# w_down in a tuned encoder block: the sums of the staying operands on VectorE, the first splits of a change behind the last bank's copy

## The chip, the cores and the metric

The kernel runs on one core of a Trainium2 chip. The metric is the device time of one execution in microseconds; the time of a kernel is the median of its runs. The core has TensorE (PE) for matrix products, VectorE (DVE), ScalarE (ACT) and GpSimd (POOL) for work on rows of elements, and SyncE (SP), which here only issues DMAs. Each engine works through its own queue in order; semaphores hold an instruction back until what it needs is there.

## The reference

One layer of an encoder: an attention group and a Fourier group share an input and an output projection, then a gated MLP follows. Everything is float32, with 2048 positions, a model width of 1024 and a hidden width of 2816. What matters here is the MLP:

```python
h = rmsnorm(x, g_ffn[l])
up = centred_dwconv(h @ w_up[l], w_conv[l], b_conv[l])
gate, val = up[..., :D_FF], up[..., D_FF:]
x = x + (jax.nn.silu(gate) * val) @ w_down[l]
return rmsnorm(x, g_final)
```

`centred_dwconv` is a convolution of width 3 over the positions, for each channel by itself.

## The kernel before

**Products of float32.** The matmuls here take operands of the type float32r. Every float32 operand is split into a high part of that type and a low part, and a product is three matmuls: high by high, high by low, low by high (`mm3`, lines 127 to 129). `split` makes the parts: line 83 copies the high part on ScalarE, line 84 subtracts it on VectorE (or on another engine that is named) to get the low part, and so follows line 83.

**The up products.** The product of 1024 columns of `h` with `w_up` is done by a scheme of Strassen's kind: blocks of two by two are combined by sums, seven products (p1, p5, p6, p2, p7, p4, p3) are made instead of eight, and their results are combined in three PSUM banks for each of the 22 steps n: bank a takes p1, p6, p7 and p4 one after the other, bank d p5 and p3, bank c p2. `exec_up` copies or adds a bank into a row buffer (`xg` for the gate, `xv` for the value) after a product, with ScalarE (line 979) and VectorE (line 980). A product that follows in the same bank must wait until the copy has read it. As a rule the order is p7 of step n, p1 of step n+1, p4 and p3 of step n; the last step of a half has no p1 behind its p7. After p4 the convolution of the value part follows, after p3 that of the gate part (lines 1007 to 1009), then `silu` and the product of the two parts (1014, 1015), which is stored to DRAM (`gd`). This is done twice: grp 0 for the first 1024 positions, grp 1 for the others.

**The w_down products.** The 22 blocks of hidden channels are shared out: blocks 0 to 9 are multiplied directly in rounds (`fil`, `exec_fil`; rnd 0 to 2, and rnd 3 at the end), the other twelve in two groups of six by the same seven-product scheme (`dn`, `exec_dn`). In a round, eight banks of PSUM collect ten steps n, each with a gate block and two weight blocks (tile `d`), 24 matmuls in a step. The sequence is: up grp 0, round 0, up grp 1, round 1, dn 0, round 2, dn 1, round 3.

**The staying operands.** In the seven-product scheme one side stays for a whole phase: seven tiles `b` (one for each product) with a high and a low part. Before up grp 1 they have to be made anew from `h` (four block rows, kb 0 to 3), before dn 0 and dn 1 from `w_down` (three block rows each). `b_part` makes one block row: four loads from DRAM into a buffer of the tag `xg` and one of the tag `xv` (two buffers each, shared with the up products' row buffers; tile `hb`), four sums (`sums` with `second=True`, lines 840 to 843: three new tiles of the tag `sum`, which has three buffers, and one sum in place), and seven splits into `b`. It is called from `exec_fil` at every second step n of the rounds 0, 1 and 2, so ten times. In the kernel before, the four sums are on GpSimd (`nc.gpsimd`), the low parts on VectorE. Two other users of `sums` have theirs on VectorE: `prep_a` and, before the first up products, `b_pieces`.

**What sets the order.** A planner puts the instructions of each engine in an order: it goes through the program with estimates of its own for durations and takes, for an engine that is free, the ready instruction that comes first in the program. On the chip the order is fixed. So an instruction whose input comes later than estimated holds up all that is behind it on its engine. `issue_after(r, prev)` adds an edge for the planner that puts `r` behind `prev`; without `wait` no semaphore is made for it.

**Operands of the rounds.** `flow` prepares operands ahead of use: nine ring buffers (`ring`), of which a step of a round takes three, so the operands of a step are written when the third step before it is done. The loads of a step need one of two stage buffers.

Of the kernel before, what the change touches and what calls it, by code (L numbers as in the profile page):

```python
# [40 lines left out]
class Block:  # L41
# [808 lines left out]
    def b_part(self, grp, kb, out):  # L850


        nc = self.nc

        st = [self.mp.tile([P, S // 2 + 3], F32, tag=tag, bufs=2, name=f"hb{grp}_{kb}{tag}")[:, :2 * HALF]
              .rearrange("p (k c) -> p k c", k=2) for tag in ("xg", "xv")]
        for half in range(2):
            if grp < 2:
                src = self.htd[kb + 4 * half, :, grp * S // 2:(grp + 1) * S // 2]
            else:  # L860
                f = self.FT + self.CH * (grp - 2) + kb + self.NK * half
                src = self.a["w_down"][f * P:(f + 1) * P, :]
            for i in range(2):
                nc.sync.dma_start(st[i][:, half], src[:, i * HALF:(i + 1) * HALF])
        x11, x21, x12, x22 = (st[i // 2][:, i % 2] for i in range(4))
        t1, t2, t3, t4 = self.sums(self.sp, (x11, x21, x12, x22), f"hs{grp}_{kb}", nc.gpsimd, True)
        for o, v in zip(out, (x11, t1, t2, x21, t3, t4, x22)):
            self.split(v, o[:, 0, kb], o[:, 1, kb])

    def b_pieces(self, out):  # L870

# [90 lines left out]
    def exec_up(self, grp, n, q, o):  # L962
        nc, p = self.nc, self.mp
        ps = self.product(q, f"u{grp}_{n}", o)
        W1 = S // 2 + 3
        at = 1 if grp == 0 else 2
        c = [slice(at, at + HALF), slice(at + HALF, at + 2 * HALF)]
        if q == "p1":
            for part, nm in enumerate(("xg", "xv")):
                f = n + NF * part  # L970
                xb = p.tile([P, W1], F32, tag=nm, bufs=2, name=f"{nm}{grp}_{n}")
                self.xb[n, nm] = xb
                if grp == 0:
                    nc.gpsimd.memset(xb[:, 0:1], 0.0)
                else:
                    nc.gpsimd.memset(xb[:, W1 - 1:], 0.0)  # L976
                    nc.gpsimd.tensor_copy(xb[:, 0:2], self.carry[:, f, :])
        xg, xv = self.xb[n, "xg"], self.xb[n, "xv"]
        copy = lambda o, i: nc.scalar.activation(o, i, AF.Copy)
        add = lambda o, i: nc.vector.tensor_tensor(o, i, o, ALU.add)  # L980
        if q == "p1":
            copy(xg[:, c[0]], ps)
        elif q == "p6":
            copy(xg[:, c[1]], ps)
        elif q == "p2":
            add(xg[:, c[0]], ps)
        elif q == "p7":
            copy(xv[:, c[1]], ps)
            add(xv[:, c[1]], self.banks[f"u{grp}_{n}", "d"])
        elif q == "p4":  # L990
            copy(xv[:, c[0]], ps)
            self.conv(grp, n, 1)
        elif q == "p3":
            add(xg[:, c[1]], ps)
            self.conv(grp, n, 0)
            self.gate(grp, n)
# [275 lines left out]
```

## Time and profile before

| | |
|---|---|
| median of three runs | 2517.06 us (2513.75 to 2518.77) |
| the profiled execution | 2513.03 us, span 2511.2 us |
| TensorE busy | 2456.5 us |
| VectorE busy | 1771.0 us |
| ScalarE busy | 1298.3 us |
| GpSimd busy | 791.8 us |

The span is the time from the first to the last instruction in the trace. Times within the trace are counted from its start. A matmul's duration in the trace is modelled, and neighbours overlap, so the distance of their starts is what tells how TensorE gets on. A row of a timeline has in brackets how long the engine was idle before the instruction and what ended that. The granted clock is a share of TensorE's full 2.4 GHz; 0.5 of it is its other level, 1.2 GHz.

### The profile page before, as it was taken

The numbers are of one execution on the slowest core, as the hardware profiler recorded it, in microseconds if no ns is written. First come the engines' busy times: TensorE is split into PE (matmuls) and PEld (weight loads), VectorE is DVE, ScalarE is ACT, GpSimd is POOL, SyncE is SP. The second block draws the span as 40 slices with busy tenths as digits, with TensorE's granted clock in tenths as the row PEclk, the third lists the DMA queues.
The fourth block names the chain that finished last, engine by engine and source line by source line (L and its number), as shares of the span: only waits on it lengthen the run. The fifth ranks groups of instructions, "written<-read, shape, count | busy, mean of one in ns | idle before, by whom it ended". The sixth has DMA issues, their size and how long they took to land.

```text
span 2511.2 us, 34985 instructions
## 1 busy us (share of the span) xinstructions
PE 2456.5 (98%) x12893; PEld 2086.4 (83%) x12893; DVE 1771.0 (71%) x2760; ACT 1298.3 (52%) x2048; POOL 791.8 (32%) x839
## 2 busy tenths in 40 slices
PE   9999998999999998998999999999999999999998
PEld 9998877888888887877888888778888887887876
DVE  4533358988888994243877777787777778767783
ACT  6322236888888885333655455545545555224242
POOL 1400014988888887332110110220100003003010
PEclk9999999999999999999999999999999999999999
DMA  8334557443232314675422222452222226666563
GB/s 271 97 119 143 154 159 211 98 77 74 42 94 41 60 35 136 211 252 172 143 76 84 93 76 77 150 195 90 76 85 93 76 78 195 228 232 223 202 222 130
DMA packets 212635, 330.65 MB, mean 132 GB/s; under 512 B 19232, under 2 KB 143472, under 8 KB 205552
## 3 DMA queue, kind: packets, MB, share of 16 engines
q1 hardware_dynamic: 151920, 244.46, 29.4%
q0 software_dynamic: 18816, 37.72, 7.1%
q10 hardware_dynamic: 41728, 46.24, 5.8%
q8 instruction: 101, 1.65, 0.3%
q14 instruction: 70, 0.57, 0.1%
HBM read 227.67 MB, written 100.70 MB: 131 GB/s over the span
## 4 chain that ended last, share of the span: by engine, by line
PE 47%; DVE 3%; DMA 2%; ACT 1%; issue 1%; POOL 1%; SPq 0%; ACTq 0%; POOLq 0%; DVEq 0%
PE pd L129 2%; PE pd L127 2%; PE pd L128 2%; DVE b L84 1%; DVE d L84 1%; PE o L128 1%; PE o L127 1%; PE o L129 1%; DMA g<-gd 1%; DMA wd<-gd 0%; PE psu_0a L127 0%; DVE r L1110 0%; PE psu_0a L129 0%; PE psu_0a L128 0%; PE psu_20a L128 0%
## 5 line engine op out<-in xcount | busy, mean ns | idle before, releaser
L592 POOL TENSOR_TENSOR z<-z,z 128x1024 f32<-128x1024 f32 x128 | 306.4, 2410 | 0.0
L570 PE MATMUL s<-k,q 128*128 128x512 f32 x1024 | 281.4, 396 | 3.0 <-DVE mn L575 2.1
L579 ACT ACTIVATE z<-z,mn 128x2048 f32<-128x2048 f32 x128 | 257.4, 2011 | 33.2 <-DVE mn L575 31.8
L570 PEld LDWEIGHTS s<-k,q 128*128 128x128 f32 x1024 | 174.4, 188 | 29.3 <-DVE mn L575 5.1
L575 DVE CUSTOM_DVE_ANT_0 z<-s,dist,mn 128x1024 f32<-128x1024 f32 x128 | 163.7, 1279 | 38.1 <-PE s L570 37.4
L84 DVE TENSOR_TENSOR at<-pt,at 128x512 fp32r<-128x512 f32 x256 | 169.7, 684 | 15.8 <-ACT at L83 15.7
L83 ACT ACTIVATE at<-pt 128x512 fp32r<-128x512 f32 x256 | 147.8, 592 | 47.1 <-PE pt L601 43.9
L127 PE MATMUL o<-at,v 128*128 128x256 f32 x512 | 162.6, 318 | 1.0 <-ACT at L83 1.0
L601 PE MATMUL pt<-ident,z 128*128 128x128 f32 x1024 | 155.8, 275 | 5.2 <-POOL z L592 3.3
L575 DVE CUSTOM_DVE_ANT_0 z<-s,dist 128x1024 f32<-128x1024 f32 x128 | 155.6, 1215 | 5.1 <-PE s L570 5.1
L601 PEld LDWEIGHTS pt<-ident,z 128*128 128x128 f32 x1024 | 124.5, 143 | 36.8 <-issue 7.5
L128 PE MATMUL o<-at,v 128*128 128x256 f32 x512 | 146.6, 286 | 0.3 <-DVE at L84 0.3
L129 PE MATMUL o<-at,v 128*128 128x256 f32 x512 | 144.2, 282 | 0.0
L128 PE MATMUL pd<-d,d 128*128 128x512 f32 x248 | 98.2, 396 | 4.4 <-DVE d L84 4.4
L976 POOL MEMSET xv<- 128x1 f32 x22 | 2.2, 99 | 314.8 <-DVE t L1009 257.0
L129 PE MATMUL pz<-hth,wt 128*128 128x512 f32 x256 | 100.5, 393 | 0.0
L128 PE MATMUL pz<-htl,wt 128*128 128x512 f32 x256 | 100.5, 392 | 0.0
L127 PE MATMUL pz<-hth,wt 128*128 128x512 f32 x256 | 100.4, 392 | 0.0
L127 PEld LDWEIGHTS o<-at,v 128*128 128x128 f32 x512 | 97.7, 191 | 2.7 <-ACT at L83 1.2
L127 PE MATMUL pd<-d,d 128*128 128x512 f32 x248 | 97.9, 395 | 0.9 <-DVE r L1110 0.8
L128 PEld LDWEIGHTS o<-at,v 128*128 128x128 f32 x512 | 97.9, 191 | 0.8 <-DVE at L84 0.5
L129 PE MATMUL pd<-d,d 128*128 128x512 f32 x248 | 97.9, 395 | 0.2
(1327 smaller groups left out, 7527.3 us busy)
## 6 DMA issues: line engine op xcount, KB each, us to landing
wu<-in_w_up SPq DMA_DIRECT2D x44, 1024.0 KB
r<-x2d SPq DMA_DIRECT2D x48, 512.0 KB
wd<-in_w_down SPq DMA_DIRECT2D x40, 512.0 KB
q<-qd POOLq DMA_DIRECT2D x32, 512.0 KB, 6.9
x2d<-r SPq DMA_DIRECT2D x32, 512.0 KB
g<-gd SPq DMA_DIRECT2D x32, 384.0 KB
gd<-t SPq DMA_DIRECT2D x22, 512.0 KB
wd<-gd SPq DMA_DIRECT2D x40, 256.0 KB
```

The source lines that it names most:

```text
L83: r = nc.scalar.activation(hi, src, AF.Copy)
L84: return r, (lo_engine or nc.vector).tensor_tensor(lo, src, hi.bitcast(F32), ALU.subtract)
L127: mm(ah, bh, start=first and i == 0, stop=False)
L128: mm(ah, bl, start=False, stop=False)
L129: r = mm(al, bh, start=False, stop=last and i == n - 1)
L570: nc.tensor.matmul(ps[:, j * HALF:(j + 1) * HALF], qt[:, 2 * c + l, i % 4 * P:i % 4 * P + P], kt[:, c, k0:k0 + HALF], start=l == 0, stop=l ...
L575: nc.vector.tensor_tensor_reduce(zt[:, half * 1024:(half + 1) * 1024], ps, dist[:, d0:d0 + 1024], SLOPES[h], 3.0e38 if half == 0 else mn[: ...
L579: nc.scalar.activation(zt, zt, AF.Exp, bias=mn[:, 2 * c + 1:2 * c + 2], scale=-1.0, accum_out=ss[:, c:c + 1])
L592: nc.gpsimd.tensor_tensor(z[:, x], z[:, x], z1[:, x], ALU.add)
L601: nc.tensor.transpose(pt[:, j * P:(j + 1) * P], zs[n, 0][:, kb * P:(kb + 1) * P], self.ident)
L976: nc.gpsimd.memset(xb[:, W1 - 1:], 0.0)
```

## The change

`b_part` takes its four sums on VectorE instead of GpSimd, in all ten calls. In the calls with kb 0 of grp 1 and grp 2, that is in the first block row of rounds 0 and 1, the seven high parts on ScalarE get an edge behind `last_copy`, the copy of p4's bank that was made last: that of step 21 of the up products before. Grp 3 (round 2, after `dn` products) gets no edge.

```diff
--- before.py
+++ after.py
@@ -863,9 +863,11 @@
             for i in range(2):
                 nc.sync.dma_start(st[i][:, half], src[:, i * HALF:(i + 1) * HALF])
         x11, x21, x12, x22 = (st[i // 2][:, i % 2] for i in range(4))
-        t1, t2, t3, t4 = self.sums(self.sp, (x11, x21, x12, x22), f"hs{grp}_{kb}", nc.gpsimd, True)
+        t1, t2, t3, t4 = self.sums(self.sp, (x11, x21, x12, x22), f"hs{grp}_{kb}", nc.vector, True)
         for o, v in zip(out, (x11, t1, t2, x21, t3, t4, x22)):
-            self.split(v, o[:, 0, kb], o[:, 1, kb])
+            r, _ = self.split(v, o[:, 0, kb], o[:, 1, kb])
+            if kb == 0 and grp < 3:
+                self.issue_after(r, self.last_copy)
 
     def b_pieces(self, out):
 
@@ -988,7 +990,7 @@
             copy(xv[:, c[1]], ps)
             add(xv[:, c[1]], self.banks[f"u{grp}_{n}", "d"])
         elif q == "p4":
-            copy(xv[:, c[0]], ps)
+            self.last_copy = copy(xv[:, c[0]], ps)
             self.conv(grp, n, 1)
         elif q == "p3":
             add(xg[:, c[1]], ps)
```

## Rows read from the trace of the kernel before

**Rows 1.** The profile page, busy time of the engines over the span: us, share of the span, instructions.

```profile
PE 2456.5 (98%) x12893; PEld 2086.4 (83%) x12893; DVE 1771.0 (71%) x2760; ACT 1298.3 (52%) x2048; POOL 791.8 (32%) x839
```

**Rows 2.** The list of TensorE's waits from 1500 us to the end, longest in total first: who waited, for whom, us in total, times, the longest.

```profile
PE psu_21a L127 <- ACT xv L979: 5.1, 2, 2.7
PE pd L128 <- DVE d L84: 4.4, 3, 2.4
```

**Rows 3.** The timeline of TensorE in change 1: start, duration (us), engine, line, operation, tile, shape, count, and in brackets the idle time before it with what ended it. `psu_21a` is the bank of p7 and then of p4, `psu_21d` that of p3, `pd` a bank of the staying rounds.

```profile
1608.00 0.39 PE L129 MATMUL psu_21a<-b,aup_21p 128*128 128x512 f32 x1
1608.22 0.39 PE L127 MATMUL pd<-d,d 128*128 128x512 f32 x1
...
1609.13 0.39 PE L128 MATMUL pd<-d,d 128*128 128x512 f32 x1
1611.88 0.50 PE L127 MATMUL psu_21a<-b,aup_21p 128*128 128x512 f32 x1 [2.36 <-ACT xv L979]
1612.21 0.39 PE L128 MATMUL psu_21a<-b,aup_21p 128*128 128x512 f32 x1
...
1614.52 0.39 PE L129 MATMUL psu_21a<-b,aup_21p 128*128 128x512 f32 x1
1615.26 0.50 PE L127 MATMUL psu_21d<-b,aup_21p 128*128 128x512 f32 x1 [0.35 <-DVE xv L980]
```

**Rows 4.** The timeline of ScalarE in change 1; line 83 is a split's high part, line 979 the copy of a bank (p7's at 1611.24, p4's at 1614.94).

```profile
1607.57 0.63 ACT L83 ACTIVATE b<-hb_0xg 128x512 fp32r<-128x512 f32 x1 [1.24 <-DMA hb_0xg<-htd]
...
1610.71 0.63 ACT L83 ACTIVATE b<-hs_t 128x512 fp32r<-128x512 f32 x1 [0.52 <-POOL hs_t L841]
1611.24 0.58 ACT L979 ACTIVATE xv<-psu_21a 128x512 f32<-128x512 f32 x1
...
1614.94 0.60 ACT L979 ACTIVATE xv<-psu_21a 128x512 f32<-128x512 f32 x1 [1.93 <-PE psu_21a L129]
```

**Rows 5.** The timelines of TensorE (p4's first matmul, p3's first) and of ScalarE (p7's copy) in change 2.

```profile
2093.90 0.50 PE L127 MATMUL psu_21a<-b,aup_21p 128*128 128x512 f32 x1 [2.73 <-ACT xv L979]
...
2097.29 0.50 PE L127 MATMUL psu_21d<-b,aup_21p 128*128 128x512 f32 x1 [0.36 <-DVE xv L980]
...
2093.26 0.58 ACT L979 ACTIVATE xv<-psu_21a 128x512 f32<-128x512 f32 x1
```

**Rows 6.** The timelines of TensorE and of VectorE in change 1, towards the end of the staying rounds; line 84 is a split's low part.

```profile
1658.40 0.55 PE L128 MATMUL pd<-d,d 128*128 128x512 f32 x1 [2.44 <-DVE d L84]
...
1662.15 0.39 PE L127 MATMUL pd<-d,d 128*128 128x512 f32 x1
...
1655.87 0.68 DVE L84 TENSOR_TENSOR b<-hb_3xg,b 128x512 fp32r<-128x512 f32 x1
1656.47 0.68 DVE L84 TENSOR_TENSOR b<-hb_3xv,b 128x512 fp32r<-128x512 f32 x1
```

**Rows 7.** Three stretches of 10 us of change 1: length, busy us (and instructions) of PE, PEld, DVE, ACT, POOL, then the granted TensorE clock, the DMA share and GB/s.

```profile
1640.00:1650.00 10.00, 10.00 (x46) 8.29 (x45) 10.00 (x11) 4.10 (x8) 7.37 (x8) 1.00 0.62 209
1650.00:1660.00 10.00, 7.30 (x28) 5.09 (x27) 10.00 (x11) 6.58 (x12) 5.84 (x6) 0.94 0.40 137
1660.00:1670.00 10.00, 10.00 (x41) 8.17 (x40) 7.05 (x12) 3.46 (x6) 2.33 (x2) 0.89 0.84 288
```

**Rows 8.** The timelines of TensorE and of VectorE in change 3, and the stretch of 10 us behind the wait, with columns as in group 7.

```profile
2273.90 0.50 PE L127 MATMUL pd<-d,d 128*128 128x512 f32 x1 [0.77 <-DVE r L1110]
...
2298.57 0.49 PE L128 MATMUL pd<-d,d 128*128 128x512 f32 x1 [1.71 <-DVE d L84]
...
2303.99 0.39 PE L127 MATMUL pd<-d,d 128*128 128x512 f32 x1
...
2285.33 2.40 DVE L84 TENSOR_TENSOR d<-wd,d 128x512 fp32r<-128x512 f32 x2
...
2296.77 2.95 DVE L84 TENSOR_TENSOR d<-wd,d 128x512 fp32r<-128x512 f32 x3
...
2300.00:2310.00 10.00, 10.00 (x38) 8.11 (x38) 7.59 (x13) 3.77 (x7) 0.00 (x0) 0.83 0.86 288
```

**Rows 9.** The timelines of POOL (a sum) and of VectorE (a low part of `b`) at the same time in change 1, and of the tile of the sums the row of line 843 where it runs on VectorE, in the first part of the layer (shortest, median and longest of four, ns).

```profile
1653.65 1.74 POOL L843 TENSOR_TENSOR hs_t<-hb_3xg,hs_t 128x512 f32<-128x512 f32 x1
...
1652.46 1.78 DVE L84 TENSOR_TENSOR b<-hb_3xg,b 128x512 fp32r<-128x512 f32 x1
...
L843 DVE TENSOR_TENSOR hs_t<-hb,hs_t x4: 680/686/987, 1102.9 to 1129.0; 128x512 f32<-128x512 f32 x4
```

**Rows 10.** One stretch of change 1, first for the instructions of the tile `b` alone, then for those of the tile `d` alone: length, busy us (and instructions) of PE, PEld, DVE, ACT, then the granted clock, the DMA share and GB/s.

```profile
1608.20:1659.50 51.30, 6.23 (x25) 4.35 (x24) 28.85 (x27) 16.30 (x28) 0.99 0.64 202
...
1608.20:1659.50 51.30, 39.99 (x171) 32.13 (x171) 14.80 (x18) 12.07 (x21) 0.99 0.64 202
```

**Rows 11.** The timeline of POOL: sums that waited for a load, in change 1, change 2 and change 3; and of VectorE in change 3, an add of a last product.

```profile
1639.74 1.83 POOL L841 TENSOR_TENSOR hs_t<-hb_2xv,hs_t 128x512 f32<-128x512 f32 x1 [2.91 <-DMA hb_2xv<-htd]
...
2105.08 3.81 POOL L840 TENSOR_TENSOR hs_t<-hb_1xv,hb_1xg 128x512 f32<-128x512 f32 x1 [9.00 <-DMA hb_1xv<-in_w_down]
...
2266.70 1.83 POOL L841 TENSOR_TENSOR hs_t<-hb_0xv,hs_t 128x512 f32<-128x512 f32 x1 [1.07 <-DMA hb_0xv<-in_w_down]
...
2282.71 1.31 POOL L840 TENSOR_TENSOR hs_t<-hb_1xv,hb_1xg 128x512 f32<-128x512 f32 x1 [11.22 <-DMA hb_1xv<-in_w_down]
...
2264.40 0.68 DVE L1110 TENSOR_TENSOR r<-psd_7a,r 128x512 f32<-128x512 f32 x1
```

## The prediction

> **What bounds the kernel now.** I read the page's busy shares first: TensorE is busy for 2456.5 of 2511.2 us, so all its idle time is 54.7 us and no change to the other engines can win more than that [rows 1]. The second view is the list of waits of TensorE from 1500 us on, where the gated MLP runs: only a few waits are left, 5.1 us for a ScalarE copy (two times, 2.7 us the longest) and 4.4 us for VectorE's low parts of the staying operands `d` (three times) [rows 2]. The diff touches three stretches: the change from the first half of the up products to the first w_down rounds (about 1600 to 1675 us, called change 1), the one after the second half (2085 to 2160, change 2), and the third rounds (2245 to 2320, change 3). In the timelines of these I measured what TensorE loses as the start-to-start distance of two matmuls less the 0.226 us that they stand apart when nothing waits (1608.22 after 1608.00); where a row shows a wait, that is the wait and the 0.39 us that a matmul lasts, less 0.226 [rows 3].
>
> Change 1, first place: after the product p7 six matmuls of the staying rounds run, then the product p4 must wait until p7's bank has been copied, and starts at 1611.88, 2.75 us after the sixth (1609.13). The next one is 0.33 later; p3 behind it starts 0.74 after p4's last, and its second 0.33 after that [rows 3]. Lost: 2.52 + 0.10 + 0.51 + 0.10 = 3.2 us. The cause stands in ScalarE's rows: p7 ends near 1608.4 (last start 1608.00 and 0.39), but its copy runs only at 1611.24. In the queue ahead of it lie splits of the new staying blocks (`b`): one waits 1.24 us for its load until 1607.57, another at 1610.71 has waited 0.52 us for POOL's sum, and the copy comes behind that one [rows 4]. Change 2 has the same picture: p4 starts at 2093.90 after a wait of 2.73, the copy is at 2093.26, and p3 waits as long as in change 1 (0.36 us for line 980, there 0.35) [rows 3, 5]. Lost, with the other three terms as in change 1: 2.89 + 0.10 + 0.51 + 0.10 = 3.6 us.
>
> Change 1, second place: at 1658.40 TensorE has waited 2.44 us for VectorE's low part of `d`; the eighth matmul after that starts at 1662.15, 3.75 us later where 8 x 0.226 would be 1.8, with the granted clock down to 0.94 and 0.89 in those slices: the time is lost first to the wait and then to 1.2 instead of 2.4 GHz [rows 6, 7]. Lost: 2.6 in the wait and 1.9 after it, 4.5 us. VectorE is busy for all of 1640 to 1660 [rows 7]. Change 3: a wait of 1.71 us for the same low parts at 2298.57, with 0.83 as the granted clock in the slice after it [rows 8]; lost in the same way, 1.9 in the wait, and 2.2 in the 14 matmuls up to 2303.99 that take 5.4 us instead of 3.2: 4.1 us. Together 15.4 us stand in the places that the diff touches.
>
> **The change part by part.** *The order on ScalarE.* In changes 1 and 2 the seven high parts of the first block row (0.62 us each) go behind the last bank's copy, that of p4. p4 needs p7's copy, so nothing of them can be ahead of p7's copy any more. That one can then start when p7 ends (1608.4) and be done at 1609.0; six matmuls of the staying rounds last until 1609.36 anyway, so p4 starts without a wait. For p3 the add of line 980 must be done before p4 ends, 2.7 us later; VectorE reaches it behind the four sums (from the landing at 1607.6 on, four at 0.6 us each) at 1610.1, in time. Worth 3.2 + 3.6 = 6.8 us; if only the copies' waits go and p3's stay, 2.6 + 3.0 = 5.6. Who waits for the seven delayed splits? Their low parts on VectorE, the two buffers of the block row (the loads of the third row follow the first row's last low part), and at last the up products behind the rounds. p4's copy (1614.94 now [rows 4]) comes 2.7 us earlier, so that the splits can follow from 1612.8 on; p4's end and the convolution steps behind it, which they share the two engines with, come earlier by as much. Cost taken: nothing; if that cover is gone, the second place of change 1 is late by as much.
>
> *The sums.* 40 tensor-by-tensor instructions leave POOL (16 in change 1, 12 in each of the others) and go to VectorE. On POOL one takes 1.3 to 1.8 us [rows 11], and a low part beside it takes 1.78 us instead of 0.68; on VectorE the same sum took 0.69 us in the first part of the layer [rows 6, 9]. From 1608.2 to 1659.5 in change 1 the 27 low parts of `b` keep VectorE for 28.85 us and the 18 of `d` for 14.80, 43.65 us together [rows 10]. With nothing beside them 45 low parts and 16 sums take 61 x 0.60 = 36.6 us, at the distance at which low parts follow each other when POOL rests (1655.87, 1656.47) [rows 6]: 7.0 us to the good. If whole durations counted instead, it would be 45 x 0.68 + 16 x 0.69 = 41.6, only 2.0 to the good. For the second place of change 1 the low part must come 2.6 us earlier than now, and 3.2 more since TensorE is earlier by that: 5.8. With 7.0 the wait goes and all 4.5 us come back; with 2.0 it is late by 3.8 instead of 2.6, and 1.2 us are lost on top. I take 3.5, near the first figure, since VectorE has no idle time there and distances are what counts; a good fifth is left out for loads that land late.
>
> The Trainium skill, VectorE: DVE Perf Modes, section The DRAIN you can't avoid, says that after every VectorE instruction the next doesn't start until the pipeline has emptied. Taken as whole durations end to end that makes the 2.0 and not the 7.0 the right figure, and the sum below 11.5 - 3.5 - 1.2 = 6.8 us instead of 11.5; the rows at 0.60 us start to start with 0.68 us of duration speak against it.
>
> In change 3 VectorE starts, from 2285.33 until the last of three at 2296.77 is done (2299.7), five low parts of `d` and six of `b` in 14.3 us [rows 8]; at 0.60 us, with eight sums, these are 11.4. The low part is late by 1.9 us there: it would come 2.9 earlier. The gain is between nothing (the loads decide) and 4.1; I take 2.6, two thirds.
>
> *What is added.* VectorE's queue now holds the sums' waits for their loads. POOL waited 1.07 us for the second half of a load in change 3 (until 2266.70), at a time when VectorE had line 1110's add at 2264.40 to do, on which a last product's bank hangs; it waited 11.2 us for a later one, 9.0 in change 2, 2.9 in change 1 [rows 11]. If the sum stands ahead of the add of 2264.40, that add comes 2.9 us late (2266.70 and 0.60, for 2264.40). Bounds: nothing (the planner puts the adds first) to 4.0 us with a second such place; I take 1.4, half of the one place. No DMA is added or moved; POOL's queue loses its sums, and behind them stand only edge columns.
>
> Sum: 3.2 + 3.6 + 3.5 + 2.6 - 1.4 = 11.5 us. TensorE works without another wait of this size until the end [rows 2], so the end comes earlier by as much. The profiled execution took 2513.03 us (span 2511.2); 2501.5 would follow. The median of the three runs is 2517.06, 4 us above it; against the median the forecast is 2505.6. With the best of each bound the gain is 15.4 + 0.8 (a wait at 2273.90 in change 3 for line 1110, on the same queue [rows 8]) = 16.2, with the worst 5.6 - 1.2 + 0 - 4.0 = 0.4: 2500.9 to 2516.7.
>
> **The rivals.** (1) VectorE becomes the bound: its low parts of `d` wait behind sums and low parts of `b`, the second place of change 1 loses 1.2 us more, that of change 3 keeps its loss, and the full 4.0 us of new waits come in. 6.8 - 1.2 - 4.0 = 1.6: 2515.5, not to be told from no change. For it: no idle time in 1640 to 1660 [rows 7]; against it: what POOL's neighbourhood costs the low parts now [rows 10].
>
> (2) Slower: VectorE stands still for a load. The staying operands of a round may be written two rounds ahead (a round is 24 matmuls, 5.4 us), hi and low parts of one take 1.7 + 1.9 us, so some 7.3 us of slack stand behind a sum; where a sum waits longer than that with low parts of `d` behind it, TensorE waits. In change 3 POOL waited 11.2 us for a load, in change 2 9.0: 3.9 + 1.7 us pass through; in change 1 VectorE has no slack, and the 2.9 us pass through whole; each of three such waits costs 1.9 us more at the lower clock. 3.9 + 1.7 + 2.9 + 5.7 = 14.2, less the 6.8 that the order brings, and no gain at the second places: 7.4 us slower, 2524.5. Against it: ScalarE's splits wait for the same loads now, and VectorE waits behind those already.
>
> (3) The change doesn't do what it says: the planner sets something else ahead of p7's copy that waits, and half of the 6.8 us stays lost. 3.4 + 3.5 + 2.6 - 1.4 = 8.1 if all else holds, 2509.0; with the gains at the second places halved, 5.1, 2512.0.
>
> **How the numbers follow.** A measurement of this kernel can tell about 0.2%, 5.0 us, from no change. Forecast 0.66, all of it faster by more than that; rival 1 0.16, no change; rival 2 0.10, slower; rival 3 0.08, half faster, half no change. Faster 0.70, within 0.2% 0.20, slower 0.10. The predicted time is the forecast's, 2505.6. The range goes from 2499, the best bound with two microseconds of scatter (the runs before stand up to 3.3 from their median), to 2516, which takes in rivals 1 and 3; rival 2 and a few hundredths on either side stay out.
>
> **What would show it.** Right: p7's copy starts within 0.1 us of p7's end in both changes and no wait stands at p4; the low parts of `b` and `d` last 0.68 us throughout; POOL is nearly idle in the three changes; the granted clock stays at 1.0 there; no wait for `d` above 1 us. Wrong: VectorE idle for a load with low parts of `d` behind it; new waits of TensorE for line 1110 in change 3; a wait for `d` near 1655 that is as long as now.

## The result and the profile after

The changed kernel takes 2497.92 us (median of 4 runs, 2494.53 to 2499.01); the kernel before, timed on the same chip, 2517.91 us (4 runs, 2513.75 to 2519.98). The ratio is 0.9918, with a 95% interval from 0.9906 to 0.9929: 20.0 us faster. The forecast had 11.5, and the time lies 1.1 us below the range. The profiled execution took 2498.35 us, its span is 2496.5.

TensorE's busy time on the page answers to [rows 1]; it has fallen by 7.9 us for the same 12893 matmuls. Some 4 us of that are the matmuls that ran at the lower clock behind the two waits for `d` [rows 6, 8], by the prediction's count; the rest was not traced.

```profile
PE 2448.6 (98%) x12893; PEld 2084.6 (84%) x12893; DVE 1762.3 (71%) x2800; ACT 1297.2 (52%) x2048; POOL 726.9 (29%) x799
```

The list of TensorE's waits from 1500 us on, in answer to [rows 2]: neither the copy nor the low parts of `d` stand in it; the longest that is left is 0.9 us.

```profile
PE pd L128 <- DVE b L84: 0.9, 1, 0.9
PE psd_5a L127 <- DVE r L1112: 0.8, 1, 0.8
PE pd L127 <- ACT b L83: 0.4, 1, 0.4
```

Change 1, first place, in answer to [rows 3, 4]: TensorE's timeline from p7's last matmul on, then ScalarE's. Lines behind 868 have moved down by two, so the copy is line 981 now. No bracket stands at p4 (1612.99) or at p3 (1615.81). P7's copy starts 0.43 us after p7's last matmul does, about when that one ends, and the splits of `b` stand behind p4's copy at 1616.01.

```profile
1611.86 0.39 PE L129 MATMUL psu_21a<-b,aup_21p 128*128 128x512 f32 x1
1612.09 0.39 PE L127 MATMUL pd<-d,d 128*128 128x512 f32 x1
...
1612.77 0.39 PE L127 MATMUL pd<-d,d 128*128 128x512 f32 x1
1612.99 0.44 PE L127 MATMUL psu_21a<-b,aup_21p 128*128 128x512 f32 x1
...
1615.58 0.39 PE L129 MATMUL psu_21a<-b,aup_21p 128*128 128x512 f32 x1
1615.81 0.39 PE L127 MATMUL psu_21d<-b,aup_21p 128*128 128x512 f32 x1
```

```profile
1612.29 0.60 ACT L981 ACTIVATE xv<-psu_21a 128x512 f32<-128x512 f32 x1 [2.09 <-PE psu_21a L129]
...
1616.01 0.60 ACT L981 ACTIVATE xv<-psu_21a 128x512 f32<-128x512 f32 x1 [2.60 <-PE psu_21a L129]
...
1618.15 0.62 ACT L83 ACTIVATE b<-hb_0xg 128x512 fp32r<-128x512 f32 x1
```

VectorE's timeline in change 1 (line 840 is the first of the four sums) and the stretches that answer to [rows 7]; columns as there. The sum lasts 0.68 us like the low parts, and they follow each other at 0.60. The planner has also set six low parts of `d` ahead of the third block row's sums. TensorE stays at full clock while GpSimd rests.

```profile
1641.03 3.69 DVE L84 TENSOR_TENSOR d<-wd,d 128x512 fp32r<-128x512 f32 x6
1644.64 0.68 DVE L840 TENSOR_TENSOR hs_t<-hb_2xv,hb_2xg 128x512 f32<-128x512 f32 x1
1645.24 0.68 DVE L84 TENSOR_TENSOR b<-hb_2xg,b 128x512 fp32r<-128x512 f32 x1
1645.85 0.68 DVE L841 TENSOR_TENSOR hs_t<-hb_2xv,hs_t 128x512 f32<-128x512 f32 x1
```

```profile
1640.00:1650.00 10.00, 10.00 (x45) 8.28 (x45) 8.89 (x15) 5.87 (x12) 0.00 (x0) 1.00 0.91 281
1650.00:1660.00 10.00, 10.00 (x45) 8.26 (x44) 10.00 (x18) 6.10 (x12) 0.99 (x4) 1.00 0.65 213
...
2300.00:2310.00 10.00, 10.00 (x46) 8.29 (x45) 6.40 (x14) 2.93 (x6) 0.00 (x0) 1.00 0.24 79
```

The stretch of [rows 10], for `b` and then for `d` alone: 23 low parts of `b` keep VectorE for 14.43 us (27 for 28.85 before), 23 of `d` for 14.40 (18 for 14.80 before). That is 0.63 us each where it was 1.07 and 0.82.

```profile
1608.20:1659.50 51.30, 9.74 (x42) 7.43 (x40) 14.43 (x23) 15.44 (x27) 1.00 0.81 254
...
1608.20:1659.50 51.30, 42.04 (x185) 34.90 (x186) 14.40 (x23) 13.30 (x23) 1.00 0.81 254
```

In the table below "lost" is the prediction's measure, the distance from one matmul's start to the next less 0.226 us, added up wherever a distance is over 0.26 us. The stretches are 1600 to 1690, 2083 to 2180 and 2245 to 2325. The profiled execution's time is beside it.

| kernel | change 1 | change 2 | change 3 | sum | profiled execution |
|---|---|---|---|---|---|
| before, the execution that the prediction read | 8.25 | 4.15 | 5.13 | 17.5 | 2513.03 |
| changed | 0.05 | 0.05 | 0.11 | 0.2 | 2498.35 |
| before, another execution (experiment 2) | 14.05 | 8.67 | 2.94 | 25.7 | 2523.79 |
| order alone | 7.49 | 2.15 | 3.55 | 13.2 | 2507.54 |
| sums alone | 1.30 | 1.13 | 0.00 | 2.4 | 2500.25 |
| sums alone, again | 0.72 | 0.83 | 0.00 | 1.5 | 2498.65 |
| changed, again | 0.05 | 0.06 | 0.00 | 0.1 | 2496.62 |

### The profile page after: what moved, and what is told of

It is laid out like the page before. It is cut to its first block, busy times and chain, and to the rows that moved or that the text cites. A ratio compares the mean times of both kernels' runs of the same rounds, so it can differ in the third digit from the quotient of the medians.

```text
span 2496.5 us, 34951 instructions
## 1 busy us (share of the span) xinstructions
PE 2448.6 (98%) x12893; PEld 2084.6 (84%) x12893; DVE 1762.3 (71%) x2800; ACT 1297.2 (52%) x2048; POOL 726.9 (29%) x799
## 4 chain that ended last, share of the span: by engine, by line
PE 52%; DVE 1%; DMA 1%; ACT 0%; issue 0%; POOL 0%; ACTq 0%; POOLq 0%; SPq 0%; DVEq 0%
PE pd L129 3%; PE pd L128 3%; PE pd L127 3%; PE o L127 1%; PE o L128 1%; PE o L129 1%; PE psu_0a L127 0%; PE psu_0a L128 0%; PE psu_0a L129 0%; DVE r L1112 0%; DMA g<-gd 0%; PE psu_21a L127 0%; PE psu_21a L129 0%; PE psu_19a L129 0%; PE psu_17a L128 0%
## 5 line engine op out<-in xcount | busy, mean ns | idle before, releaser
L127 PEld LDWEIGHTS o<-at,v 128*128 128x128 f32 x512 | 97.7, 191 | 2.5 <-ACT at L83 1.0
L128 PEld LDWEIGHTS o<-at,v 128*128 128x128 f32 x512 | 98.1, 192 | 0.8 <-DVE at L84 0.5
L129 PEld LDWEIGHTS o<-at,v 128*128 128x128 f32 x512 | 97.4, 190 | 0.0
```

The costliest lines, as they stand in the source:

```text
L127: mm(ah, bh, start=first and i == 0, stop=False)
L128: mm(ah, bl, start=False, stop=False)
L129: r = mm(al, bh, start=False, stop=last and i == n - 1)
```

## The experiments

The diffs are against the changed kernel. Theory: GpSimd's sums slowed VectorE's low parts, and nearly all that was lost in the three changes hung on that and on splits that waited for the sums. Rivals: it was the order on ScalarE; GpSimd's hold on buffers; or a freak of one execution.

### 1. Each part alone

The order alone takes the sums back to GpSimd; the sums alone take the edge away.

```diff
-        t1, t2, t3, t4 = self.sums(..., nc.vector, True)
+        t1, t2, t3, t4 = self.sums(..., nc.gpsimd, True)
```

> The sums stay on GpSimd; only the edge behind the last bank's copy is added. If the two parts of the change act each by itself, the waits at p4 and p3 in changes 1 and 2 go (6.8 us of the trace's 16) and the waits for the low parts of d in changes 1 and 3 stay (4.5 and 4.1 us): 6 to 8 us faster than before. The rival is that the order is worth little without the sums, because the first splits then come later while the sums still slow VectorE: the wait at 1658 grows by the 3 us that TensorE is earlier, and the gain is 3 to 4 us.

```diff
-            r, _ = self.split(v, o[:, 0, kb], o[:, 1, kb])
-            if kb == 0 and grp < 3:
-                self.issue_after(r, self.last_copy)
+            self.split(v, o[:, 0, kb], o[:, 1, kb])
```

> The sums are on VectorE, without the edge. If each part acts by itself, the waits for d go and those at p4 and p3 stay at 6.8 us: 9 to 11 us faster than before. The rival is that p7's copy was late mostly because the splits ahead of it waited for GpSimd's sums (0.8 and 0.5 us and the slowed parts): with sums on VectorE the copy runs about 1.4 us earlier, 3 us of the 6.8 come back too, and it is 13 us faster.

The order alone: 2512.09 us (8 runs), ratio 0.9973 [0.9961, 0.9984] to the kernel before (2519.19), so 7.1 us faster by the medians, within the 6 to 8 expected. The waits at p4 and p3 are gone, but the low parts still run beside GpSimd's sums. Here are VectorE's rows in change 1, and the two of TensorE's waits that come of them: the low parts take 1.75 to 1.78 us where GpSimd works, 0.64 each in the pair behind. TensorE comes to them earlier than before: behind p4 and p3, 7.4 us are lost in change 1, where the kernel before lost 5.0 in the execution that the prediction read and 8.2 in the other.

```profile
1650.38 1.78 DVE L84 TENSOR_TENSOR b<-hb_2xv,b 128x512 fp32r<-128x512 f32 x1
1652.08 1.77 DVE L84 TENSOR_TENSOR d<-wd,d 128x512 fp32r<-128x512 f32 x1
1653.78 1.75 DVE L84 TENSOR_TENSOR b<-hb_3xg,b 128x512 fp32r<-128x512 f32 x1
1655.46 1.28 DVE L84 TENSOR_TENSOR d<-wd,d 128x512 fp32r<-128x512 f32 x2
```

```profile
1653.91 0.49 PE L128 MATMUL pd<-d,d 128*128 128x512 f32 x1 [0.51 <-DVE d L84]
1656.19 0.74 PE L129 MATMUL pd<-d,d 128*128 128x512 f32 x1 [1.79 <-DVE d L84]
```

The sums alone: 2499.71 us (4 runs), ratio 0.992 [0.9903, 0.9936], so 19.5 us faster. Both expectations, 9 to 11 and 13, were too low. The second places are gone, and so is most of the first. In change 1 two splits of `b` still run ahead of p7's copy and wait for their loads (1.25 us until 1611.22, 0.64 before the one shown), but none waits for a sum. ScalarE's rows, then the wait of p4 that is left:

```profile
1612.49 0.63 ACT L83 ACTIVATE b<-hb_0xg 128x512 fp32r<-128x512 f32 x1 [0.64 <-DMA hb_0xg<-htd]
1613.03 0.61 ACT L83 ACTIVATE b<-hs_t 128x512 fp32r<-128x512 f32 x1
1613.55 0.58 ACT L979 ACTIVATE xv<-psu_21a 128x512 f32<-128x512 f32 x1
```

```profile
1614.18 0.50 PE L127 MATMUL psu_21a<-b,aup_21p 128*128 128x512 f32 x1 [1.03 <-ACT xv L979]
```

So 7.1 and 19.5 are not parts of 20.0 that add up: both take away the wait for p7's copy. The order alone takes the splits away from in front of it, the sums alone take the wait for GpSimd out of those splits.

To see what the edge is worth on top of the sums, the two kernels were timed in one call, in five rounds.

> The sums on VectorE without the edge for the first splits, timed beside the changed kernel in the same call. Theory (the edge is worth what the trace of the sums alone still loses in the first places, 1.30 and 1.13 us in the first two changes, against 0.05 in the changed kernel): 2.4 us slower than the changed kernel, 2498 to 2502. Rival (the edge is worth as much as without the sums, some 6 us, as the prediction credited it): 2503 to 2506. Rival (the edge is worth nothing once VectorE isn't slowed): within 1 us of the changed kernel.

> The changed kernel once more, beside the sums alone: 2496 to 2499 by median, and in its profile under 0.3 us lost in each of the three changes of stage. If its losses scatter from run to run as those of the kernel before do (17.5 and 25.7 us in two profiled executions), waits of 2 us and more show up in one of them.

Sums alone 2498.65 us, ratio 0.9927 [0.9915, 0.994]; the changed kernel 2496.62, ratio 0.9918 [0.9905, 0.9932], both to 2516.56. The edge is worth 2.0 us by the medians, near the 2.4 of the first expectation, and 1.4 by the losses of the two traces (1.5 less 0.1): without it p4 still waits for p7's copy, here in change 1 and in change 2.

```profile
1610.63 0.50 PE L127 MATMUL psu_21a<-b,aup_21p 128*128 128x512 f32 x1 [0.45 <-ACT xv L979]
...
2084.76 0.50 PE L127 MATMUL psu_21a<-b,aup_21p 128*128 128x512 f32 x1 [0.55 <-ACT xv L979]
```

The intervals of the two ratios overlap, so the times alone don't exclude that the edge is worth nothing. They do exclude that it is worth 6 us on top of the sums: no run of the one kernel is more than 5.5 us from a run of the other. The changed kernel lost 0.1 us in the three changes.

### 2. The kernel before, once more

> The kernel before once more, for a second trace. Its profiled execution was 4 us below its median, while that of the changed kernel was at its median. If the rest of the gain (20 us by the medians, 14.7 by the spans of the two traces) is made of waits in the three changes that differ from run to run, this trace shows 2 to 6 us more lost there than the first (at p4 in change 2 the granted clock stays up in the first trace, after a wait longer than the one in change 1 that brings it down). If it is scatter elsewhere, the three changes lose the same 16 to 17 us and the difference stands in other stretches.

2518.52 us (10 runs, 2515.19 to 2523.79), ratio 0.9994 [0.9982, 1.0005]. Its profiled execution, 2523.79, is 10.8 us longer than the one that the prediction read, and 25.66 - 17.53 = 8.1 us of that stand in the three changes, more than the 2 to 6 expected: 5.4 at p4 and p3 with the slow matmuls behind them, 2.7 in the waits further on, most of them for `d` (change 3 lost less than in the first). ScalarE's timeline up to p7's copy in change 1, TensorE's from p4 on, and the stretch:

```profile
1611.04 0.63 ACT L83 ACTIVATE b<-hb_0xg 128x512 fp32r<-128x512 f32 x1 [2.84 <-DMA hb_0xg<-htd]
1612.48 0.63 ACT L83 ACTIVATE b<-hs_t 128x512 fp32r<-128x512 f32 x1 [0.81 <-POOL hs_t L840]
...
1614.16 0.63 ACT L83 ACTIVATE b<-hs_t 128x512 fp32r<-128x512 f32 x1 [0.53 <-POOL hs_t L841]
1614.69 0.58 ACT L979 ACTIVATE xv<-psu_21a 128x512 f32<-128x512 f32 x1
```

```profile
1615.33 0.50 PE L127 MATMUL psu_21a<-b,aup_21p 128*128 128x512 f32 x1 [3.94 <-ACT xv L979]
...
1616.45 0.63 PE L128 MATMUL psu_21a<-b,aup_21p 128*128 128x512 f32 x1
1616.88 0.63 PE L129 MATMUL psu_21a<-b,aup_21p 128*128 128x512 f32 x1
```

```profile
1610.00:1620.00 10.00, 6.06 (x20) 4.52 (x19) 7.99 (x7) 4.06 (x8) 6.83 (x5) 0.83 0.51 140
```

It is the same chain as in [rows 4], a load, a sum, a split, the copy. But p7 ended earlier against the load, so p4 waited 3.94 us and not 2.36, and the matmuls behind it stand 0.43 us apart: the clock fell to the lower level, which it had not done at this place in the first execution. The same place that the prediction priced at 3.2 us cost 4.1 here for p4's first matmul alone (1615.33, after 1610.99), and 0.2 us more for each of the slow ones up to 1619.79, 5.8 us in all.

### 3. What GpSimd's work costs VectorE

The first of these gives GpSimd four subtractions in each block row that nobody uses; they read the block row's buffers.

```diff
             if kb == 0 and grp < 3:
                 self.issue_after(r, self.last_copy)
+        for v in (x11, x22, x11, x22):
+            nc.gpsimd.tensor_tensor(self.beside, v, self.beside, ALU.subtract)
```

> The changed kernel, and in each of the ten block rows four further subtractions on GpSimd of the sums' shape, which read the block row and a tile of their own that nothing uses: GpSimd is as busy as before, but nobody waits for what it makes. If the low parts were slow because GpSimd works beside them, they take 1.3 to 1.8 us again while it works, the sums too, and VectorE, which has more to do than before, falls behind: 8 to 15 us slower than the changed kernel. If the gain came from the splits no longer waiting for GpSimd's results, the low parts may be slow, but the kernel stays within 3 us of the changed one.

2526.08 us (10 runs), ratio 1.002 [1.0008, 1.0032] to the kernel before, 26 us slower than the changed kernel by the ratios and 28 by the medians, where 8 to 15 were expected. All the sums are on VectorE, and it is slower than before. VectorE's rows, GpSimd's beside them (line 872 is the added one), and the longest of TensorE's waits:

```profile
1636.99 1.78 DVE L840 TENSOR_TENSOR hs_t<-hb_1xv,hb_1xg 128x512 f32<-128x512 f32 x1
1638.70 1.78 DVE L84 TENSOR_TENSOR b<-hb_1xg,b 128x512 fp32r<-128x512 f32 x1
1640.40 0.68 DVE L841 TENSOR_TENSOR hs_t<-hb_1xv,hs_t 128x512 f32<-128x512 f32 x1
```

```profile
1636.60 1.63 POOL L872 TENSOR_TENSOR beside<-hb_1xv,beside 128x512 f32<-128x512 f32 x1
1638.31 1.62 POOL L872 TENSOR_TENSOR beside<-hb_2xg,beside 128x512 f32<-128x512 f32 x1
```

```profile
1650.44 0.80 PE L128 MATMUL pd<-d,d 128*128 128x512 f32 x1 [4.27 <-DVE d L84]
```

These subtractions also hold the block row's buffers against the next loads. So two more kernels give GpSimd work on a tile of its own, each piece behind the high part of every second split: one subtraction, or three memsets, which read nothing. (The diffs here leave out the lines that make the tile `beside` and that count the splits as `j`.)

```diff
+            if j % 2 == 0:
+                g = nc.gpsimd.tensor_tensor(self.beside, self.beside, self.beside, ALU.subtract)
+                self.issue_after(g, r, True)
```

> The changed kernel with four more GpSimd subtractions in each block row of w_down, on a tile that nothing else uses, each behind the high part of every second split. Theory (GpSimd's work beside VectorE's two-input work slows both, as the profile of the run with GpSimd beside VectorE has it: 1.78 us for a low part, 0.68 without): low parts and sums under them take 1.3 to 1.8 us, waits for low parts come back in the first two changes, slower than the changed kernel by 8 to 28 us (2506 to 2526). Rival (what cost 28 us there was that GpSimd held the block row's buffers, so that the next loads started late): nothing is held here, so within 3 us of the changed kernel (2495 to 2501), and no wait for low parts.

```diff
+            if j % 2 == 0:
+                for _ in range(3):
+                    g = nc.gpsimd.memset(self.beside, 0.0)
+                    self.issue_after(g, r, True)
```

> The same places as the run with subtractions on a tile of GpSimd's own, with three memsets of 0.52 us at each, which write a tile and read none. Theory A (it is GpSimd's reading of SBUF that slows VectorE's instructions with two SBUF inputs): low parts stay at 0.68 us and the time within 3 us of the changed kernel (2495 to 2501). Theory B (any GpSimd work does): low parts at 1.3 to 1.8 us as with the subtractions, 2506 to 2526.

The subtractions: 2514.23 us (10 runs, 2508.24 to 2519.09), ratio 0.9981 [0.9969, 0.9994]. That is 16 us slower than the changed kernel, with no buffer held. Four of GpSimd's take 5.82 us together, 1.45 each, and VectorE's rows beside them start 1.45 us apart; then TensorE waits for `d`. The timeline, engine by engine:

```profile
1637.34 1.53 DVE L84 TENSOR_TENSOR b<-hb_1xg,b 128x512 fp32r<-128x512 f32 x1
1638.79 1.52 DVE L84 TENSOR_TENSOR b<-hb_1xv,b 128x512 fp32r<-128x512 f32 x1
1640.24 1.52 DVE L84 TENSOR_TENSOR b<-hs_t,b 128x512 fp32r<-128x512 f32 x1
...
1636.84 5.82 POOL L872 TENSOR_TENSOR beside<-beside 128x512 f32<-128x512 f32 x4 [5.92 <-ACT b L83]
...
1644.46 0.53 PE L128 MATMUL pd<-d,d 128*128 128x512 f32 x1 [3.36 <-DVE d L84]
```

The memsets: 2496.95 us (4 runs), ratio 0.9912 [0.9889, 0.9934], as fast as the changed kernel, though GpSimd is busy for seven microseconds on end; VectorE's low parts beside it last 0.69 and start 0.60 apart, as the two timelines show:

```profile
1636.85 0.69 DVE L84 TENSOR_TENSOR b<-hb_1xg,b 128x512 fp32r<-128x512 f32 x1
1637.45 0.69 DVE L84 TENSOR_TENSOR b<-hb_1xv,b 128x512 fp32r<-128x512 f32 x1
...
1636.32 6.96 POOL L873 MEMSET beside<- 128x512 f32 x12 [6.54 <-ACT b L83]
```

So it is GpSimd's reading of SBUF, not its being busy, that slows VectorE's instructions with two inputs from there. The Trainium skill, SBUF — State Buffer, section Who interferes with whom, states this rule: a VectorE instruction with two SBUF inputs contends with a GpSimd instruction that reads SBUF, and not with one that only writes. The three traces agree (1.78, 1.52 and 0.69 us).

That it takes two inputs from SBUF shows in the kernel before itself. VectorE's add of a product has one input in a bank of PSUM and one in SBUF; here is one of change 3 that runs while GpSimd makes a sum (line 843):

```profile
2269.74 1.75 POOL L843 TENSOR_TENSOR hs_t<-hb_0xg,hs_t 128x512 f32<-128x512 f32 x1
...
2270.25 0.68 DVE L1110 TENSOR_TENSOR r<-psd_7a,r 128x512 f32<-128x512 f32 x1
```

In the three changes of five profiles (both of the kernel before, the order alone, and the two kernels with added subtractions) twelve such adds lie wholly within subtractions of GpSimd's, and all last 0.68 to 0.69 us. What stays open is whether GpSimd's reading is all of it: subtraction and memset differ in more than that, and another GpSimd instruction that reads a whole tile was not tried.

The 10 to 12 us between the two kernels with subtractions were not told apart further; in the slower one the low parts last longer (1.78 for 1.52), and the buffers are held as well.

### 4. What the sums cost where they now stand

Four more sums in each block row (some are made twice or three times, the results are the same; the diff leaves out how `twice` is handed down), and none at all. In the second the four sums are left out, so that the products of these rounds and phases are made from the blocks themselves.

```diff
-        tt(t1, x21, x11, ALU.subtract)
-        tt(t2, x22, t1, ALU.subtract)
+        for _ in range(2 if twice else 1):
+            tt(t1, x21, x11, ALU.subtract)
+            tt(t2, x22, t1, ALU.subtract)
         tt(x21, x22, x21, ALU.subtract)
-        tt(t4, x12, t2, ALU.subtract)
+        for _ in range(3 if twice else 1):
+            tt(t4, x12, t2, ALU.subtract)
```

> The changed kernel with four more sums on VectorE in each block row of w_down (t1 and t2 twice, t4 three times; the results are the same). Four by 0.60 us is 2.4 us a block row, 9.6 us in a stretch of four. The prediction's first rival (VectorE becomes the bound) has its point of decision here: VectorE was busy 8.9 to 9.1 of 10 us in two of the three stretches of 1630 to 1660 of the changed kernel and 10.0 in the third, so with 2.4 us more a block row of some 11 us it can't keep pace, and waits for low parts come: 5 to 20 us slower (2503 to 2518). If VectorE has room that those rows don't show (loads, not VectorE, set its pace), within 3 us (2495 to 2501).

```diff
-        t1, t2, t3, t4 = self.sums(..., nc.vector, True)
+        t1, t2, t3, t4 = x11, x21, x12, x22
```

> The changed kernel with the four sums of each block row of w_down left out (the splits take the blocks themselves, so the products are not those of the reference): what the sums still cost where they now stand. Theory (they are covered): within 2 us of the changed kernel (2496 to 2500). Rival (VectorE's work still sets when low parts are ready, or the loads' buffers come free later through it): 3 to 8 us faster (2490 to 2495).

None: 2497.12 us (4 runs), ratio 0.9912 [0.989, 0.9934]. The sums are covered where they stand: leaving them out saves 0.8 us by the medians, less than the runs scatter. Twice as many: 2503.76 us (4 runs), ratio 0.9937 [0.9914, 0.9961], 5.8 us slower by the medians, and the traces show 4.1 and 2.4 us lost in changes 1 and 2 and none in change 3. The waits are for low parts of `d`, as TensorE's list from 1500 us on shows:

```profile
PE pd L128 <- DVE d L84: 4.5, 4, 1.4
```

So VectorE has room for the four sums of a block row, but not for eight, in changes 1 and 2; the first rival begins to hold between the two.

## Why the prediction was right or wrong

**The order on ScalarE** (6.8 us): right as a mechanism. P7's copy starts when p7 ends, nothing waits at p4 and p3, and nobody waits for the seven delayed splits. That the part by itself measured 7.1 us is in part luck: at p4 and p3 the order alone takes away 6.8 us of the execution that the prediction read but 12.2 of the other, and behind them VectorE is as slow as it was, so that 7.4 us are lost there in change 1 and not 5.0. What the prediction missed is that the sums by themselves take most of the same loss away, for the splits ahead of the copy no longer wait for GpSimd. On top of them the order is worth some 1.4 to 2.0 us.

**The second places** (3.5 of 4.5, and 2.6 of 4.1): right in mechanism, too small. Distances were what counted, as it chose: 0.60 us for sums and low parts alike. By the Trainium skill, VectorE: DVE Perf Modes, section The DRAIN you can't avoid, as the prediction weighed it, whole durations would have counted, for a gain of 6.8; the trace speaks against that use of it. The section itself adds that a next instruction that isn't held starts earlier, which the prediction left out. The "good fifth" and the third left out for late loads, 2.5 us together, were not lost: VectorE waits for the first block row's load in change 1 for 0.74 us (until 1612.11), and TensorE for nothing there.

**New waits** (-1.4): did not come. The planner put low parts of `d` ahead of sums whose loads come late (1641.03 above), and change 3 lost 0.11 us in all, so no add there came late. That this order is why rival 2 did not come is read from the rows, not tried.

**The size**, and the step that failed. 11.5 with the 3.9 us of discounts is 15.4. The measure of the table finds 17.5 in the execution that the prediction read: 2.1 lie in places it saw and left out (the wait at 2273.90 in its upper bound) or did not add up. All 17.5 went, to within 0.2. The profiled execution would then be 2495.5; it was 2498.35, and the median 2497.92. TensorE's wait for line 711 before 1600 us, outside what the diff touches, was 10.8 us in it, 7.6 in the kernel before's; over twelve profiles it lies between 7.6 and 8.8 with the sums on GpSimd and between 9.2 and 10.9 with VectorE's or none, and why is open. The 2.4 us by which the median stands above 2495.5 are no more than the rest of the kernel scatters by: less the table's sums, the two executions of the kernel before leave 2495.5 and 2498.1 us, those of the changed kernel 2498.1 and 2496.5. So, as far as these four show, the gain stands in the three changes and nowhere else.

The prediction's first bound, that no more than TensorE's 54.7 us of idle time can be won, is not one: of the 14.7 us between the two spans, 7.9 came out of TensorE's busy time.

The failed step is "the median of the three runs is 2517.06, 4 us above it; against the median the forecast is 2505.6". It carried the gap over as a constant that the change doesn't touch. Experiment 2 shows where such gaps lie: three quarters of 10.8 us between two executions stood in the three changes, 5.4 of the 8.1 us in longer waits at p4 and p3 with the lower clock behind them. The change takes that away too. So the 20.0 us are 11.5, and 3.9 of discounts, and 2.1 not added up, and 4.9 by which the execution read was shorter than the median (2517.91), less 2.4 lost elsewhere. That the 4.9 lie mainly in the changes is taken over from experiment 2's pair, since only profiled executions show it. The range failed with it: its lower end put the same 4 us on top. Taken from the execution that was read, the prediction's best bound would have been 2513.03 - 16.2 = 2496.8 us, and the measured 2497.92 lies above that.

**The rivals.** VectorE as the bound needs more than the four sums (experiment 4). VectorE standing still for a load did not happen at a price, and the planner set nothing ahead of p7's copy.

## What to carry to other kernels

A sum that GpSimd does "for free" beside VectorE is not free if GpSimd reads SBUF while VectorE's instruction has both its inputs there: compare the durations of one VectorE instruction with and without a GpSimd row beside it, and if they differ as 1.78 and 0.68 do, moving the work onto VectorE can shorten VectorE's own queue (1771.0 us busy before, 1762.3 after, with 40 instructions more). When a loss is a wait with a fall of the clock behind it, its size in one profiled execution is one draw; take the gap between that execution and the median as part of the same loss until a second profile says otherwise. Price two edits that act on one wait together, not as a sum.

## What the runs showed of the hardware

Not expected was that the two engines fall into step: beside VectorE's low parts GpSimd's subtractions on a tile of its own take 1.45 us each, and the low parts start 1.45 us apart, so the two proceed at the same pace, where low parts alone start 0.60 us apart; 12 memsets in 6.96 us cost VectorE nothing. Nor was it expected that the same wait, at the same place of the same program, is followed by full clock in one execution (p4 after 2.36 us, matmuls 0.23 us apart) and by 1.2 GHz in another (after 3.94 us, 0.43 us apart until 1619.79). The length of the wait alone doesn't tell which: in the first of the two, 2.73 us in change 2 [rows 5] were followed by full clock (p3 starts 3.39 us after p4, in change 1 3.38), and 1.71 us in change 3 by the lower one [rows 8]. Nor was it expected that a kernel without such waits is also a steadier one: 2495.99 to 2499.04 in five runs, for 2515.19 to 2523.79 in ten.
